# Hybrid decoder trunk on one core: order of a head's score matmuls, and the queues of the first loads

## Chip, cores, metric

The kernel runs on one core of one Trainium2 chip. Its time is the device time of one launch in microseconds (us). Lower is better. The engines are called as in the profile: PE is the matrix engine (TensorE), PEld its weight loads, DVE the vector engine, ACT the scalar engine, POOL is GpSimd, SP the queue engine that issues most DMAs. A line number L927 is a line of the kernel before; the changed kernel has the same lines two or three further down.

## Reference

Two layers of a decoder trunk on x of 512 tokens by 1024. A layer projects RMSNorm(x) once and feeds four branches: a short gated convolution (A), sparse attention with an indexer and top-k (B), a gated linear recurrence in chunks (C), and cross-attention into 256 memory tokens (M). Each branch is lifted to 1024 columns, gated, summed, projected and added to x; a SwiGLU feed-forward follows. What the change touches is the start, where the memory tokens are normed and projected, and the scores inside the recurrence:

```python
def hgrn2_chunkwise(q, k, v, log_f):            # 4 heads, chunks of 64 tokens
    ...
    cum = jnp.cumsum(gc, axis=3)
    ref = cum[:, :, :, HG_CHUNK // 2 - 1:HG_CHUNK // 2, :]
    ...
    a_intra = jnp.einsum('nbhtk,nbhsk->nbhts', qc * jnp.exp(cum - ref), kc * jnp.exp(ref - cum))
    o_intra = jnp.einsum('nbhts,nbhsv->nbhtv', jnp.where(tri, a_intra, 0.0), vc)
    ...
def reference(x, mem, ...):
    mem_n = rmsnorm(mem, mem_norm)
    ...
    mk, mv = jnp.split(mem_n @ mem_w_kv, 2, axis=-1)     # in each layer
```

## The kernel before

**Products.** All large products are made from operands split in two (hi and lo), with three matmuls each: hi by hi (L260), hi by lo (L261), lo by hi (L262). A weight chunk (class Chunk, L212 to L226) is loaded by SP into w_raw, 1 MB for 1024 rows of 256 columns. There are two such buffers. ACT copies it to w_hi (L97 through L224) and DVE subtracts to w_lo (L225), in two halves of 128 by 1024.

**Order.** The order in which engines run their instructions is decided at build time by a scheduler of the tile framework, from dependencies, priorities and estimated times. Each engine then runs its own list strictly in that order. All helpers for ACT are recorded under L97. DMA completions are counted on a small set of semaphores, eight of them for the DMAs of SP and ACT together, handed out in turn; a DMA that gets one in use waits until the earlier DMA on it has landed.

**Start.** SP loads the memory tokens mem_in in one DMA (L150). Parameter rows (norm gains, convolution weights, bounds) are gathered in one tile called rows (L151 to L157): three sets are loaded by ACT's queue (norm_mix, norm_ffn, mem_norm), five by SP's (conv_w, lower bounds, three head norms). Then PE transposes rows once (L160) and ACT copies the result to prm (L161), which holds every gain as a column. Before that PE runs 14 warm-up matmuls (L144).

mem_in_T (L372 to L384) transposes the memory tokens tile by tile (L376), and ACT and DVE write them, scaled by the gain from prm, as mt_hi and mt_lo (L377, L378). ACT squares mem_in for the norm (mem_sq, L381). first_h (L388 to L415) loads x in two halves (xin, L391), squares its four token tiles (mem_sq, L397), and transposes it (L410). mem_kv (L417 to L458) makes keys and values from mt and four weight chunks of a layer; for a chunk and each of two token tiles it runs eight k tiles of three matmuls. It norms keys (L438) and transposes them (L442). The start runs mem_in_T, then mem_kv of layer 0 interleaved with first_h, then mem_kv of layer 1.

**Recurrence.** For each of four heads (function head, L873 to L968) ACT and DVE form the scaled operands, and then PE makes the scores of four 128-token tiles in one PSUM bank pa. A tile holds two chunks of 64. The 128 by 128 product within chunks is L927; the 64 by 64 block between the first chunk of a tile and the second is L928, which overwrites a corner of the same tile:

```python
925  for t in range(NT):
926      s = slice(t * P, (t + 1) * P)
927      pe.matmul(pa[:, s], z[:, s], cmr[:, s], start=True, stop=True)
928      pe.matmul(pa[0:CH, t * P + CH:(t + 1) * P], k_mid[:, t, :], q_mid[:, t, :], start=True, stop=True)
```

These are plain fp32 matmuls, which the profile shows as two passes, each with its weight load. DVE then copies the scores under the causal mask (L930). Behind that stand transposes of the keys (L934), the state updates (L940) and the outputs (L952, L954). The heads are interleaved with logits and with the lift of branch B by a script (L970), so PE has large products between these steps. In attention, L705 multiplies on two half tiles of 64 columns, one in each half of the array.

Of the kernel before, what the change touches and what calls it, by code (L numbers as in the profile page):

```python
# [21 lines left out]
P = 128  # L22
S = 512
NT = S // P
D = 1024
# [44 lines left out]
def hybrid_trunk(ctx: ExitStack, tc: tile.TileContext, x, mem, positions, norm_mix, w_in, conv_w,  # L70
                 dsa_q_norm, dsa_k_norm, hgrn_lower_bounds, hgrn_out_norm, mem_norm, mem_w_kv,
                 mem_q_norm, mem_k_norm, w_lift, w_out, norm_ffn, ffn_w_up, ffn_w_down, out):
    nc = tc.nc
# [29 lines left out]
    def mm_ps():  # L103
        return pmm.tile([P, 512], F32, name="mm")
# [40 lines left out]
    rows = sp.tile([P, P], F32, name="rows")  # L145
# [1 line left out]
    warm = consts.tile([P, 1], F32, name="warm")  # L147
    A(warm, one, AF.Exp)
    mem_in = sp.tile([P, 2, D], F32, name="mem_in")
    nc.sync.dma_start(mem_in, mem[0].rearrange("(t p) d -> p t d", p=P))  # L150
    for lo, src in ((0, norm_mix.rearrange("l (c p) -> (l c) p", p=P)),  # L151
                    (16, norm_ffn.rearrange("l (c p) -> (l c) p", p=P)),
                    (32, mem_norm.rearrange("(c p) -> c p", p=P)),
                    (40, conv_w.rearrange("l w (c p) -> (l w c) p", p=P)),
                    (64, hgrn_lower_bounds.rearrange("l (c p) -> (l c) p", p=P)),
                    (72, hgrn_out_norm), (74, mem_q_norm), (76, mem_k_norm)):
        (nc.scalar if lo < 40 else nc.sync).dma_start(rows[lo:lo + src.shape[0], :], src)  # L157
    prm = consts.tile([P, n_rows], F32, name="prm")
    ps = tr_ps()
    pe.transpose(ps[:, :n_rows], rows[:n_rows, :], ident[:n_rows, :n_rows])  # L160
# [19 lines left out]
    for l in range(DEPTH):  # L180
        a = sp.tile([P, HD], F32, name=f"gq_raw{l}")
# [57 lines left out]
    def pair(a, k, s=slice(None)):  # L239
        return a[0][:, k, s], a[1][:, k, s]  # L240

    def features(w, a, js, k0=0, kt=None, pss=None):
        """Feature-major products of the 128-column tiles js of a chunk."""
        kt = w.kt if kt is None else kt
        pss = [mm_ps() for _ in js] if pss is None else pss
        for ks, _, _ in w.parts:
            for j, ps in zip(js, pss):
                for k in ks:
                    mm3(ps, w.tile(k, j), pair(a, k0 + k), k0 + k == 0, k0 + k == kt - 1)
        return pss  # L250
# [6 lines left out]
    def mm3(ps, a, b, first, last):  # L257
        ah, al = a
        bh, bl = b
        pe.matmul(ps, ah, bh, start=first, stop=False)  # L260
        pe.matmul(ps, ah, bl, start=False, stop=False)  # L261
        pe.matmul(ps, al, bh, start=False, stop=last)  # L262
# [228 lines left out]
    def mixer(l, h, norms, cm, cf):  # L491
# [11 lines left out]
        def lift(n, y, merged, last=None):  # L503
            def gates(m):
                gw = wchunk(w_in[l][:, C_GATE + n * D + m * P:C_GATE + n * D + (m + 2) * P], KD, 256)
                gs = [gate_tile()[:, :S] for _ in range(2)]
                for g, ps in zip(gs, features(gw, h, (0, 1))):
                    with tc.high_priority(offset=AHEAD):
                        dve.tensor_mul(g, ps, r_b)
                    sigmoid(g, g, mix.tile([P, S], F32, name="gate_e", bufs=1))  # L510
                return gs

            look = LOOK[l][n] == "1"
            ahead = gates(0) if look else None
            for m in range(0, KD, 2):
                if look:
                    gs, ahead = ahead, gates(m + 2) if m + 2 < KD else None
                else:
                    gs = gates(m)
                lw = wchunk(w_lift[l, n][:, m * P:(m + 2) * P], 4, 256)  # L520
                pls = features(lw, y, (0, 1))
                for i in range(2):
                    g, pl = gs[i], pls[i]
                    with tc.high_priority(offset=AHEAD):
                        if n == 3:
                            dve.tensor_mul(merged[:, m + i, :], g, pl)
                        else:
                            dve.tensor_mul(g, g, pl)
                            dve.tensor_add(merged[:, m + i, :], merged[:, m + i, :], g)
                    if last is not None:  # L530
                        last(m + i)
                yield
# [26 lines left out]
        def conv_branch(y):  # L559
            for c2 in range(2):  # L560
                us = [gate_tile(), gate_tile()]
                w = wchunk(w_in[l][:, C_AX + c2 * 256:C_AX + (c2 + 1) * 256], KD, 256)
                for u, ps in zip(us, features(w, h, (0, 1))):
                    pool.memset(u[:, 0:2], 0.0)
                    with tc.high_priority(offset=AHEAD):
                        dve.tensor_mul(u[:, 2:], ps, r_b)
                yield
                w = wchunk(w_in[l][:, C_AC + c2 * 256:C_AC + (c2 + 1) * 256], KD, 256)
                for j, ps in enumerate(features(w, h, (0, 1))):
                    c, u = 2 * c2 + j, us[j]  # L570
                    v = gate_tile()[:, :S]
                    with tc.high_priority(offset=AHEAD):
                        dve.tensor_mul(v, ps, r_b)
                    dve.tensor_mul(u[:, 2:], u[:, 2:], v)
                    A(v, u[:, 0:S], AF.Copy, scale=g_conv(l, 0, c))
                    dve.scalar_tensor_tensor(v, u[:, 1:S + 1], g_conv(l, 1, c), v, op0=OP.mult, op1=OP.add)
                    dve.scalar_tensor_tensor(u[:, 2:], u[:, 2:], g_conv(l, 2, c), v, op0=OP.mult, op1=OP.add)
                    dve.tensor_mul(u[:, 2:], u[:, 2:], r_b)
                yield
                w = wchunk(w_in[l][:, C_AB + c2 * 256:C_AB + (c2 + 1) * 256], KD, 256)  # L580
                for j, ps in enumerate(features(w, h, (0, 1))):
                    c, u = 2 * c2 + j, us[j][:, 2:]
                    with tc.high_priority(offset=AHEAD):
                        dve.tensor_mul(u, u, ps)
                    A(y[0][:, c, :], u, AF.Copy)
                    dve.tensor_sub(y[1][:, c, :], u, f(y[0][:, c, :]))
                yield
# [255 lines left out]
        with pool_("hgrn") as hp:  # L843
# [14 lines left out]
            def tmp(name, bufs=HB):  # L858
                return hp.tile([P, S], F32, name=name, bufs=bufs)
# [13 lines left out]
            def head(hh):  # L873
# [51 lines left out]
                for t in range(NT):  # L925
                    s = slice(t * P, (t + 1) * P)
                    pe.matmul(pa[:, s], z[:, s], cmr[:, s], start=True, stop=True)  # L927
                    pe.matmul(pa[0:CH, t * P + CH:(t + 1) * P], k_mid[:, t, :], q_mid[:, t, :], start=True, stop=True)  # L928
                am = a_buf[hh % 2]
                dve.copy_predicated(am, tri[:, None, :].to_broadcast([P, NT, P]),  # L930
# [31 lines left out]
                y, a = tmp("ls"), tmp("ks")  # L962
# [5 lines left out]
                yield  # L968

            script(HG[l], {"z": logits(), "H": chain(*(head(hh) for hh in range(4))), "l": lift(1, y_b, merged)})  # L970
        hvs.close()

# [132 lines left out]
```

## Time and profile before

| | |
|---|---|
| median of three timed runs | 2059.01 us (2058.93 to 2060.22) |
| the profiled execution | span 2057.1 us from first to last instruction; no other time of it is given |
| PE busy | 2046.8 us, 99% of the span |
| PE weight loads busy | 1731.1 us, 84% |
| DVE, ACT busy | 1270.5 us (62%), 1017.1 us (49%) |
| DMA | 203.83 MB, mean 99 GB/s |
| mean granted PE clock | 0.999 |

In the profile's lines an instruction is shown with its line, engine, what it writes and reads, partitions by elements, and times in us, or ns where a mean of one is meant. "x6" is a row of six merged ones: the first start, and the time to the end of the last. An arrow in square brackets names what ended the engine's idle time before it. The waits view sums such idle time: us in total, times, the longest. In the view by stretches each engine's busy time and count stand in order PE, PEld, DVE, ACT, POOL, then PE's granted clock, the share of the DMA engines and GB/s. PE's rows overlap, since matmuls are pipelined: the step from one start to the next is what one costs in a row.

### The profile page before, as it was taken

What the parts mean: (1) busy time and instruction counts of PE and PEld (TensorE: products, weight loads), DVE (VectorE), ACT (ScalarE), POOL (GpSimd) and SP (SyncE); (2) the same over time, 40 slices, a digit from 0 to 9 for tenths busy, and PEclk for the clock granted to TensorE, in tenths of its full rate; (3) what the DMA queues carried; (4) which work ended last, traced back from release to release, by engine and by line L of the source; (5) the groups of instructions that cost most, each with busy time, mean ns of one, the idle gap of its engine ahead of it and who ended that gap; (6) DMA issues with size and microseconds to landing.
All of it is one profiled execution on the core that took longest, in us unless ns stands there. A gap on an engine that the chain in (4) does not pass through costs nothing.

```text
span 2057.1 us, 27077 instructions
## 1 busy us (share of the span) xinstructions
PE 2046.8 (99%) x10588; PEld 1731.1 (84%) x10588; DVE 1270.5 (62%) x2513; ACT 1017.1 (49%) x1836; POOL 9.8 (0%) x33
## 2 busy tenths in 40 slices
PE   8999999999999999999999999999999999999999
PEld 8998988888888888888889898888888888888889
DVE  6779998547676544334457899953766754532542
ACT  7654655856665423223355456576657643322321
POOL 0000000000000000000000000000000000000000
PEclk9999999999999999999999999999999999999999
DMA  7632222212233232232242223321223332322322
GB/s 255 215 95 86 72 89 93 81 53 92 82 113 113 83 102 92 92 114 92 87 154 93 88 75 97 97 66 62 83 82 109 116 102 83 103 93 92 103 72 93
DMA packets 190783, 203.83 MB, mean 99 GB/s; under 512 B 4270, under 2 KB 182528, under 8 KB 190528
## 3 DMA queue, kind: packets, MB, share of 16 engines
q1 hardware_dynamic: 186944, 193.56, 29.2%
q10 hardware_dynamic: 3552, 8.41, 1.1%
q8 instruction: 83, 1.36, 0.3%
q14 instruction: 44, 0.36, 0.1%
q0 software_dynamic: 160, 0.13, 0.0%
HBM read 191.60 MB, written 10.49 MB: 98 GB/s over the span
## 4 chain that ended last, share of the span: by engine, by line
PE 98%; DMA 1%; DVE 0%; ACT 0%; SPq 0%; issue 0%; DVEq 0%; ACTq 0%
PE mm L261 30%; PE mm L260 30%; PE mm L262 30%; PE tr L705 1%; PE tr L699 1%; PE at L676 1%; PE at L675 1%; PE at L927 1%; DMA w_raw<-in_mem_w_kv_dram 1%; PE at L928 0%; PE at L260 0%; PE at L262 0%; PE at L261 0%; PE at L952 0%; PE tr L643 0%; PE tr L744 0%
## 5 line engine op out<-in xcount | busy, mean ns | idle before, releaser
L261 PE MATMUL mm<-h_lo,w_hi 128*128 128x512 f32 x1664 | 652.1, 392 | 0.0
L260 PE MATMUL mm<-h_hi,w_hi 128*128 128x512 f32 x1664 | 651.8, 392 | 0.0
L262 PE MATMUL mm<-h_hi,w_lo 128*128 128x512 f32 x1664 | 649.5, 391 | 0.0
L225 DVE TENSOR_TENSOR w_lo<-w_raw,w_hi 128x1024 fp32r<-128x1024 f32 (+1 forms) x348 | 419.7, 1207 | 350.7 <-ACT w_hi L97 349.5
L97 ACT ACTIVATE w_hi<-w_raw 128x1024 fp32r<-128x1024 f32 (+1 forms) x348 | 363.5, 1046 | 469.6 <-PE mm L261 416.8
L261 PEld LDWEIGHTS mm<-h_lo,w_hi 128*128 128x128 f32 x1664 | 312.6, 188 | 64.9 <-issue 2.5
L262 PEld LDWEIGHTS mm<-h_hi,w_lo 128*128 128x128 f32 x1664 | 312.4, 188 | 65.1 <-issue 1.4
L260 PEld LDWEIGHTS mm<-h_hi,w_hi 128*128 128x128 f32 x1664 | 312.6, 188 | 64.5 <-issue 2.0
L262 PE MATMUL mm<-w_hi,h_lo 128*128 128x256 f32 (+1 forms) x448 | 128.0, 286 | 0.0
L261 PE MATMUL mm<-w_lo,h_hi 128*128 128x256 f32 (+1 forms) x448 | 126.8, 284 | 0.0
L260 PE MATMUL mm<-w_hi,h_hi 128*128 128x256 f32 (+1 forms) x448 | 126.8, 285 | 0.0
L261 PE MATMUL mm<-a_lo,w_hi 128*128 128x512 f32 x272 | 106.1, 390 | 0.0
L260 PE MATMUL mm<-a_hi,w_hi 128*128 128x512 f32 x272 | 105.9, 389 | 0.0
L262 PE MATMUL mm<-a_hi,w_lo 128*128 128x512 f32 x272 | 105.6, 390 | 0.0
L260 PE MATMUL mm<-y_hi,w_hi 128*128 128x512 f32 x256 | 101.3, 397 | 0.0
L262 PE MATMUL mm<-y_hi,w_lo 128*128 128x512 f32 x256 | 100.2, 392 | 0.0
L261 PE MATMUL mm<-y_lo,w_hi 128*128 128x512 f32 x256 | 100.1, 391 | 0.0
L262 PEld LDWEIGHTS mm<-w_hi,h_lo 128*128 128x128 f32 x448 | 85.6, 191 | 1.4 <-issue 0.8
L260 PEld LDWEIGHTS mm<-w_hi,h_hi 128*128 128x128 f32 x448 | 85.2, 191 | 1.2 <-issue 0.8
L261 PEld LDWEIGHTS mm<-w_lo,h_hi 128*128 128x128 f32 x448 | 85.5, 191 | 0.6
L97 ACT ACTIVATE a_hi<-fg 128x512 fp32r<-128x512 f32 x44 | 27.8, 633 | 109.0 <-DVE fg L1054 109.0
L97 ACT ACTIVATE prob<-prob,small 128x128 f32<-128x128 f32 (+3 forms) x128 | 69.2, 555 | 15.2 <-DVE small L688 14.6
(351 smaller groups left out, 3048.6 us busy)
## 6 DMA issues: line engine op xcount, KB each, us to landing
w_raw<-in_w_in_dram SPq DMA_DIRECT2D x72, 1024.0 KB, 5.0
w_raw<-in_ffn_w_up_dram SPq DMA_DIRECT2D x44, 1024.0 KB, 5.1
w_raw<-in_w_lift_dram SPq DMA_DIRECT2D x32, 512.0 KB, 3.4
w_raw<-in_ffn_w_down_dram SPq DMA_DIRECT2D x16, 1024.0 KB, 5.0
w_raw<-in_mem_w_kv_dram SPq DMA_DIRECT2D x8, 1024.0 KB, 5.2
w_raw<-in_w_out_dram SPq DMA_DIRECT2D x8, 1024.0 KB, 4.9
kv<-kv ACTq DMA_DIRECT2D x8, 512.0 KB, 7.4
xT<-x_spill SPq DMA_DIRECT2D x16, 256.0 KB, 5.8
```

The costliest lines, as they stand in the source:

```text
L97: i = act.activation(dst, src, func, **kw)
L225: dve.tensor_sub(lo, raw[:, k:e], f(hi))
L260: pe.matmul(ps, ah, bh, start=first, stop=False)
L261: pe.matmul(ps, ah, bl, start=False, stop=False)
L262: pe.matmul(ps, al, bh, start=False, stop=last)
L675: pe.matmul(ps, q[:, hh, s], k[0][:, :n], start=True, stop=False)
L676: pe.matmul(ps, q[:, hh, s], k[1][:, :n], start=False, stop=True)
L699: pe.transpose(pp[:, (2 * e + i) * P:(2 * e + i + 1) * P], probs[2 * i + e][:, b * P:(b + 1) * P], ident)
L705: pe.matmul(pv[e * HD:(e + 1) * HD, :], vt[:, b, :], pt[:, b, e * 2 * P:(e + 1) * 2 * P], start=b == 0, stop=b == t)
L927: pe.matmul(pa[:, s], z[:, s], cmr[:, s], start=True, stop=True)
```

## The change

The memory tokens are loaded in two DMAs of 512 columns each. Of the parameter rows, ACT's queue now loads five sets (two more: conv_w and the lower bounds) and GpSimd's queue three (the head norms); SP loads none. In the recurrence, a head's four 128-column score matmuls come first, then its four of 64. A docstring is dropped.

```diff
     mem_in = sp.tile([P, 2, D], F32, name="mem_in")
-    nc.sync.dma_start(mem_in, mem[0].rearrange("(t p) d -> p t d", p=P))
+    for hf in range(2):
+        cs = slice(hf * D // 2, (hf + 1) * D // 2)
+        nc.sync.dma_start(mem_in[:, :, cs], mem[0][:, cs].rearrange("(t p) d -> p t d", p=P))
     for lo, src in ((0, norm_mix.rearrange("l (c p) -> (l c) p", p=P)),
                     (16, norm_ffn.rearrange("l (c p) -> (l c) p", p=P)),
                     (32, mem_norm.rearrange("(c p) -> c p", p=P)),
                     (40, conv_w.rearrange("l w (c p) -> (l w c) p", p=P)),
                     (64, hgrn_lower_bounds.rearrange("l (c p) -> (l c) p", p=P)),
                     (72, hgrn_out_norm), (74, mem_q_norm), (76, mem_k_norm)):
-        (nc.scalar if lo < 40 else nc.sync).dma_start(rows[lo:lo + src.shape[0], :], src)
+        (nc.scalar if lo < 72 else nc.gpsimd).dma_start(rows[lo:lo + src.shape[0], :], src)
...
                 for t in range(NT):
                     s = slice(t * P, (t + 1) * P)
                     pe.matmul(pa[:, s], z[:, s], cmr[:, s], start=True, stop=True)
+                for t in range(NT):
                     pe.matmul(pa[0:CH, t * P + CH:(t + 1) * P], k_mid[:, t, :], q_mid[:, t, :], start=True, stop=True)
```

Because the scheduler decides the order, the edits at the start also move instructions that they do not name. In the built changed program the lists of PE, ACT and DVE differ from those before in the first 70 us and, slightly, in the recurrence stages; between these they are the same.

## Prediction

> **What bounds the kernel now.** I read the page first, then TensorE's waits, then the first 25 us of the timeline, then the stretch around the score matmuls.
>
> ```profile
> span 2057.1 us, 27077 instructions
> PE 2046.8 (99%) x10588; PEld 1731.1 (84%) x10588; DVE 1270.5 (62%) x2513; ACT 1017.1 (49%) x1836; POOL 9.8 (0%) x33
> ```
>
> The waits of TensorE over the whole span (engine, who waited for whom, us in total, times, longest):
>
> ```profile
> PE tr L160 <- DMA rows<-in_mem_k_norm_dram: 1.9, 1, 1.9
> PE mm L261 <- DVE w_lo L225: 1.3, 2, 0.8
> PE tr L144 <- DVE ones_d L118: 1.1, 1, 1.1
> PE tr L376 <- DVE mt_lo L378: 0.9, 2, 0.6
> PE mm L260 <- ACT w_hi L97: 0.8, 1, 0.8
> ```
>
> These five are all, and each lies in the first 63 us. From 22 us on TensorE is the bound: microseconds taken out of its queue there shorten the kernel one for one, and a start that is later by some amount moves everything behind it by that amount. So the change has two places: eight blocks of score matmuls (four heads, two layers) in the bound part, and the start.
>
> **The scores.** One block, from its first matmul to what follows it (start, length, instruction; each fp32 matmul is two passes):
>
> ```profile
> 464.63 0.38 PE L927 MATMUL at<-cmr,zf 128*128 128x128 f32 x2
> 465.20 0.49 PE L927 MATMUL at<-cmr,zf 128*128 128x128 f32 x2
> 465.62 0.33 PE L928 MATMUL at<-q_mid,k_mid 128*64 128x64 f32 x2
> 465.88 0.38 PE L927 MATMUL at<-cmr,zf 128*128 128x128 f32 x1
> 467.23 0.55 PE L934 MATMUL tr<-ident,ks 128*128 128x128 f32 x3
> L928 PE MATMUL at<-q_mid,k_mid x64: 222/246/270, 464.9 to 1579.2; 128*64 128x64 f32 x64
> ```
>
> The block takes 467.23 - 464.63 = 2.60. A pair inside it repeats every 465.88 - 465.20 = 0.68: 0.42 for two 128-column passes, 0.26 for two of 64. The second 64 pass ends at 465.95 and lasts at least 0.222, so it starts 0.11 after the first and 0.15 before the next 128 pass. What do such passes cost in a row of their own kind?
>
> ```profile
> 472.63 0.83 PE L940 MATMUL tr<-hv,kst 128*128 128x128 f32 x6
> 414.67 1.08 PE L705 MATMUL tr<-pt,vt 128*64 128x256 f32 x8
> 422.57 1.52 PE L705 MATMUL tr<-pt,vt 128*64 128x256 f32 x12
> ```
>
> Six 128 passes: about 0.28 for the last one leaves 0.55 for five steps, 0.11 each, half of the 0.21 in the mixed order. In the third and second rows, passes on 64-column tiles, four more passes cost 1.52 - 1.08 = 0.44; they run two at a time, so 0.22 a step for 256 columns, twice the 0.11 for 128. Time goes with the columns, so in a row the weight loads lie behind the running passes, for 64-column tiles too. What the mixed order pays is a switch at every change of width: the next load starts only when the last pass has drained.
>
> Grouped, a block is: seven steps of 0.11, the switch 0.21, then for the eight 64 passes a first step of 0.11, six of 0.055 (half of the 128 step; no row shows 64 columns in a row) and 0.15 to switch back: 0.77 + 0.21 + 0.11 + 0.33 + 0.15 = 1.57. That saves 1.03 a block, **8.2 us** for eight. Upper price: if each 64 step keeps its 0.11, the block is 1.90 and the saving 0.70, 5.6 us. The mask copy L930, which waits for the last score, starts no later than before, and TensorE waits for nobody in these stages, so I count the saving in full.
>
> The Trainium skill, "TensorE: Matmul & The Clock Gate", Part 3, says that a weight load overlaps running matmuls only when the row group differs. Both kinds here use all rows, so by that rule no load would hide in either order and the saving would be nothing. The L940 and L705 rows speak against it: the same rows there, and steps without room for a load.
>
> **The start.** The chain of work and the timeline:
>
> ```profile
> 0.81 5.40 DMA mem_in<-in_mem_dram
> 8.08 11.56 DMA w_raw<-in_mem_w_kv_dram
> ```
> ```profile
> SPq L157 <- DMA mem_in<-in_mem_dram: 3.5, 1, 3.5
> ```
> ```profile
> xin<-in_x_dram SPq DMA_DIRECT2D x2, 1024.0 KB, 9.1
> gq_raw<-in_dsa_q_norm_dram POOLq DMA_DIRECT2D x2, 32.0 KB, 5.0
> ```
> ```profile
> 6.50 0.40 SPq L216 DMA_DIRECT2D w_raw<-in_mem_w_kv_dram  x1
> 7.57 0.46 SPq L391 DMA_DIRECT2D xin<-in_x_dram  x1
> 8.47 0.22 ACT L97 ACTIVATE prm<-tr 128x78 f32<-128x78 f32 x1
> 8.80 0.82 ACT L97 ACTIVATE mt_hi<-tr,prm 128x256 fp32r<-128x256 f32 x2
> 11.51 2.00 ACT L97 ACTIVATE w_hi<-w_raw 128x1024 fp32r<-128x1024 f32 x2 [0.70 <-DMA w_raw<-in_mem_w_kv_dram]
> 12.61 0.50 PE L260 MATMUL mm<-w_hi,mt_hi 128*128 128x256 f32 x2 [0.79 <-ACT w_hi L97]
> 16.85 1.06 ACT L97 ACTIVATE mem_sq<-xin 128x1024 f32<-128x1024 f32 x1
> 18.03 1.06 ACT L97 ACTIVATE mem_sq<-xin 128x1024 f32<-128x1024 f32 x1
> 19.09 0.46 ACT L97 ACTIVATE mt_hi<-tr,prm 128x256 fp32r<-128x256 f32 x1
> 22.03 0.39 PE L261 MATMUL mm<-w_lo,mt_hi 128*128 128x256 f32 x1 [0.54 <-DVE w_lo L225]
> ```
>
> SP stands 3.5 us: the last parameter row waits for mem_in (landed 6.2), and behind it are the first weight chunk (lands 11.5), the two halves of x (the second at 7.57 + 9.1 = 16.7) and the second chunk (8.08 + 11.56 = 19.6), each 1 MB. So a chunk takes 19.6 - 16.7 = 2.9 and half of x (16.7 - 11.5)/2 = 2.6. The change empties this queue: the two halves of mem_in, then these four with no row between. In line behind mem_in they land at 6.2 + 2.9 = 9.1, then 11.7, **14.3** and 17.2, some 2.4 us earlier than now. Halving mem_in itself gives nothing: the first square needs both halves.
>
> By itself that would start the products earlier. But ACT's order changes with it. In the built program prm, the one copy that turns the parameter rows into columns, no longer comes before the weight splits; it stands behind three of the four squares of x, the third of which waits for x's second half. And mt_hi, which needs prm, stands behind the fourth. So: x lands 14.3; third square, with prm 1.2 later and the fourth square at 15.6 (spacing 1.18 in the rows, prm slipped in); mt_hi 1.06 after that at 16.7; 0.46 more, and TensorE's first product is at **17.2** instead of 12.6.
>
> Behind it lie the first chunk's 48 products (two token tiles, eight k tiles, three products each) and ten transposes (0.11 each) before the second chunk:
>
> ```profile
> 15.63 0.41 PE L260 MATMUL mm<-w_hi,mt_hi 128*128 128x256 f32 x1
> 15.84 0.41 PE L261 MATMUL mm<-w_lo,mt_hi 128*128 128x256 f32 x1
> 19.77 0.28 PE L260 MATMUL mm<-w_hi,mt_hi 128*128 128x256 f32 x1
> 19.89 0.28 PE L261 MATMUL mm<-w_lo,mt_hi 128*128 128x256 f32 x1
> ```
> ```profile
> 10.00:15.00 5.00, 3.16 (x19) 2.05 (x19) 4.11 (x15) 4.30 (x11) 0.00 (x0) 0.98 1.04 406
> 15.00:18.00 3.00, 3.00 (x16) 3.00 (x16) 2.19 (x12) 2.97 (x7) 0.00 (x0) 0.50 1.06 366
> 18.00:22.00 4.00, 3.49 (x28) 3.29 (x27) 1.73 (x3) 3.86 (x8) 0.00 (x0) 0.97 1.08 339
> ```
>
> At full clock a product steps 0.12: 5.8 + 1.1 = 6.9, so the second chunk starts at 24.1 instead of 22.0, **+2.1**; its split halves have landed by then, so this is TensorE's own work. But the windows show the clock at 0.50 for some 3.4 us after TensorE's thin stretch from 6 to 12.6, with steps of 0.21, back at about 18.2, 5.6 after the restart. Before, that cost little, since TensorE waited for the second chunk anyway. Now the idle stretch is longer and nothing waits at its end. With 4.5 us (between 3.4 and 5.6) at 0.21 instead of 0.12, 4.5 x 0.43 = **+1.9**.
>
> The same page of the Trainium skill, Part 1, has the clock return after one window of about 3.4 us kept busy, the window running free; the 3.4 of the rows agrees. From it I estimate up to 6.8 us at half clock, 2.9 instead of 1.9.
>
> A later place:
>
> ```profile
> 63.90 0.47 DVE L438 TENSOR_SCALAR ku<-ku,mk_r 128x128 f32<-128x128 f32 x2
> 65.72 0.38 PE L442 MATMUL tr<-ident,ku 128*128 128x128 f32 x2
> ```
>
> Here the key transposes come 65.72 - 64.37 = 1.35 us after their operand. In the built program they stand 27 products (27 x 0.12 = 3.2 us) earlier in TensorE's queue, while their norm's steps on ACT and DVE come no earlier among the splits of h and the weights. A wait of 0 to 1.9 us takes the place of the cover; I take **+1.4**.
>
> The other edits I cost at nothing. Two more issues on ACT lie in its wait for mem_in, where the second stands for a row that lands at about 4. GpSimd's three more delay the last row to about 8 (issued near 3, 5.0 to land), and prm stands until 15 for x; if x came at 8 they would decide. Constants behind them are used far later.
>
> **Sum:** -8.2 + 2.1 + 1.9 + 1.4 = -2.8. The profiled execution's span is 2057.1, 1.9 under the median of the timed runs, 2059.0; both should move alike: **2056.2**.
>
> **Rivals.** (1) *The start costs little:* x lands half a microsecond sooner, the clock returns early (+0.7), the transposes keep their cover: 2.1 - 0.5 + 0.7 = +2.3, net -5.9, 2053.1. For it: transfers without a gap; against: the long idle stretch. (2) *64-column steps stay 0.11:* the saving is 5.6, net -0.2, 2058.8. For it: 0.11 is the one step seen for them. (3) *Slower:* grouping frees no load, because in fp32 passes of one bank they never hide; the start's +5.4 stays alone, 2064.4. It decides as soon as a grouped block keeps 1.9 of its 2.60 or more, that is, saves under 5.4 / 8 = 0.68. The L940 row makes it unlikely. (The rule of the Trainium skill quoted above would give this one.) (4) *prm does not hold the start:* products begin 2.4 us earlier as the transfers do, net -8.2 - 2.4 = -10.6, 2048.4. Against it stands ACT's built order.
>
> **Numbers.** Forecast 0.52, (1) 0.25, (2) 0.13, (3) 0.06, (4) 0.04. The forecast's own range is -5 to 0 (start +3 to +8). Leaving out (3) and (4), the range is 2052.5 to 2060.5. 0.2%, about what a measurement of this kernel can tell from no change, is 4.1 us. Faster by more: most of (1), all of (4), a fifth of the forecast: 0.35. Slower by more: (3) and a little of the rest: 0.08. Within: 0.57.
>
> **What would show it.** Right: a score block near 1.57 us, with all four L927 matmuls first; prm near 15.5 on ACT, behind the third square of x; first product near 17; clock 0.5 after it; the second chunk's products near 26; a TensorE wait at the key transposes near 65 to 70. Wrong: prm by 9 us, a block above 1.9, TensorE waits of over a microsecond anywhere behind 75 us, or times above 2060.5.

## The result, and the profile after

The changed kernel takes 2066.28 us (median of six runs, 2065.40 to 2067.20) beside 2059.61 for the kernel before (six runs, 2058.93 to 2060.59): ratio 1.0033, 95% interval 1.0022 to 1.0045. It is slower by some 6.7 us, where the prediction had 2.8 us gained and a range up to 2060.5.

TensorE's waits in the changed kernel, over the whole span (engine, who waited for whom, us in total, times, longest):

```profile
PE tr L378 <- ACT prm L97: 6.2, 1, 6.2
PE mm L262 <- ACT ku L97: 5.9, 1, 5.9
PE tr L162 <- DMA rows<-n_hgrn_lower_bounds_dram: 4.8, 1, 4.8
PE tr L444 <- DVE ku L440: 1.2, 1, 1.2
PE tr L144 <- DVE ones_d L118: 1.1, 1, 1.1
PE mm L262 <- ACT mt_hi L97: 0.7, 1, 0.7
```

Three of these rows are large, and only the first two matter. The third, for the last parameter row, ends before the first, for prm, begins. The second ends at 77 us and was in no step of the prediction.

The score block, whose predicted length was 1.57 us (timeline of TensorE in the changed kernel):

```profile
481.21 1.05 PE L929 MATMUL at<-cmr,zf 128*128 128x128 f32 x8
482.19 0.68 PE L931 MATMUL at<-q_mid,k_mid 128*64 128x64 f32 x8
482.80 0.55 PE L937 MATMUL tr<-ident,ks 128*128 128x128 f32 x3
```

From 481.21 to 482.80 it is 1.59 us, against 2.60 before. All eight blocks are alike. Groups of the two lines, with their mean in ns behind the busy time:

```profile
L929 PE MATMUL at<-cmr,zf 128*128 128x128 f32 x64 | 8.4, 274 | 0.0
L931 PE MATMUL at<-q_mid,k_mid 128*64 128x64 f32 x64 | 5.4, 228 | 0.0
```

To place the rest I match the matmuls of two traces by their order and take the difference of their starts, called lag below. Against the kernel before the lag is +6.7 us from the 100th matmul (29.5 us) to the 400th (65 us), +16.6 from the 550th on, +12.5 after the four score blocks of the first layer and +8.4 at the last matmul. So the score blocks take off 4.1 in each layer, and two places early in the span give 6.7 and 9.9. These are single executions: their spans differ by 7.7 (2064.8 and 2057.1) and the medians by 6.7. I take shares from traces and totals from medians.

The first place, on ACT and then TensorE:

```profile
14.01 1.06 ACT L97 ACTIVATE mem_sq<-xin 128x1024 f32<-128x1024 f32 x1 [1.01 <-DMA xin<-in_x_dram]
16.64 1.06 ACT L97 ACTIVATE mem_sq<-xin 128x1024 f32<-128x1024 f32 x1 [0.31 <-DMA xin<-in_x_dram]
17.70 0.22 ACT L97 ACTIVATE prm<-tr 128x78 f32<-128x78 f32 x1
18.88 0.82 ACT L97 ACTIVATE mt_hi<-tr,prm 128x256 fp32r<-128x256 f32 x2
19.38 0.58 PE L262 MATMUL mm<-w_hi,mt_hi 128*128 128x256 f32 x1 [0.73 <-ACT mt_hi L97]
```

The order is the one that the prediction read from the built program: prm behind the third square, and that behind x's second half. But x lands at 16.6 and not 14.3. Its issues on SP, and the median of their landing:

```profile
2.31 3.08 SPq L393 DMA_DIRECT2D xin<-in_x_dram  x2
```
```profile
xin<-in_x_dram SPq DMA_DIRECT2D x2, 1024.0 KB, 11.6
```

The second place, first the queues (SP and ACT), then the chain of waits, then ACT:

```profile
64.14 6.04 SPq L218 DMA_DIRECT2D w_raw<-in_w_in_dram  x2
64.67 0.34 ACTq L417 DMA_DIRECT2D x_spill<-xc  x1
```
```profile
64.14 11.39 DMA w_raw<-in_w_in_dram
76.67 0.28 ACT ku L97
77.00 0.58 PE mm L262
```
```profile
69.00 0.47 ACT L97 ACTIVATE kv<-mm,mem_r 128x256 fp32r<-128x256 f32 x1 [0.22 <-PE mm L264]
75.62 1.06 ACT L97 ACTIVATE w_hi<-w_raw 128x1024 fp32r<-128x1024 f32 x1 [6.14 <-DMA w_raw<-in_w_in_dram]
76.58 0.37 ACT L97 ACTIVATE ku<-mm 128x256 f32<-128x256 f32 x1
```

ACT's queue issues the 2 MB store of x (x_spill, L417) 0.53 us after SP issues a 1 MB weight chunk. The chunk takes 11.39 us to land (the 72 loads of in_w_in in the page have a median of 5.2). ACT's split w_hi waits 6.14 us for it. Behind the split in ACT's list stands the copy ku, and TensorE waits for that. Then the clock falls again. Stretches of the changed kernel (columns as explained above; the third figure from the end is the granted clock):

```profile
15.00:20.00 5.00, 1.30 (x5) 0.91 (x6) 1.10 (x6) 4.66 (x14) 0.00 (x0) 0.50 1.10 352
20.00:30.00 10.00, 10.00 (x68) 10.00 (x68) 6.70 (x24) 4.57 (x9) 0.00 (x0) 0.77 0.09 29
70.00:80.00 10.00, 3.93 (x18) 3.55 (x19) 4.58 (x17) 3.31 (x11) 0.52 (x1) 0.62 0.91 351
80.00:100.00 20.00, 20.00 (x116) 17.91 (x116) 13.61 (x59) 8.46 (x14) 0.67 (x3) 0.93 0.63 216
```

### The profile page after: what moved, and what is told of

Read it like the earlier page. It is cut to its first block, busy times and chain, and to the rows that moved or that the text cites. A ratio compares the mean times of both kernels' runs of the same rounds, so it can differ in the third digit from the quotient of the medians.

```text
span 2064.8 us, 27090 instructions
## 1 busy us (share of the span) xinstructions
PE 2041.5 (99%) x10588; PEld 1730.8 (84%) x10588; DVE 1271.3 (62%) x2513; ACT 1019.7 (49%) x1836; POOL 11.4 (1%) x36
## 3 DMA queue, kind: packets, MB, share of 16 engines
HBM read 191.60 MB, written 10.49 MB: 98 GB/s over the span
## 4 chain that ended last, share of the span: by engine, by line
PE 98%; DMA 1%; ACT 0%; DVE 0%; issue 0%; ACTq 0%
PE mm L262 30%; PE mm L263 30%; PE mm L264 30%; PE tr L707 1%; PE tr L701 1%; PE at L678 1%; PE at L677 1%; DMA xin<-in_x_dram 1%; DMA w_raw<-in_w_in_dram 1%; PE at L263 0%; PE at L264 0%; PE at L262 0%; PE at L955 0%; PE at L929 0%; PE tr L645 0%; PE tr L746 0%
```

## Experiments

The changed kernel has three working edits: the order of the scores, the queues of the parameter rows, and the memory tokens in halves. Each was timed beside the kernel before on the same chip.

| kernel | median, us | ratio to before, 95% |
|---|---|---|
| scores only | 2051.18 | 0.9962 (0.9950 to 0.9975) |
| both start edits, no scores | 2075.29 | 1.0077 (1.0064 to 1.0090) |
| all edits, store of x held late | 2059.72 | 1.0004 (0.9996 to 1.0013) |
| all edits, prm ordered first | 2055.55 | 0.9983 (0.9974 to 0.9992) |
| queues only | 2068.32 | 1.0042 (1.0029 to 1.0054) |
| scores and halves | 2058.88 | 0.9996 (0.9987 to 1.0005) |
| scores, store held late | 2055.43 | 0.9984 (0.9975 to 0.9993) |
| scores, another start | 2052.50 | 0.9965 (0.9952 to 0.9977) |
| scores and halves, store moved | 2052.76 | 0.9967 (0.9955 to 0.9980) |
| scores and queues | 2060.09 | 1.0002 (0.9993 to 1.0011) |
| scores, prm late | 2058.28 | 0.9995 (0.9986 to 1.0004) |

The kernel before had 2059.18 beside the first four, 2059.53 beside the next four, 2059.51 beside the last three.

**The scores alone.**

```diff
                     pe.matmul(pa[:, s], z[:, s], cmr[:, s], start=True, stop=True)
+                for t in range(NT):
                     pe.matmul(pa[0:CH, t * P + CH:(t + 1) * P], k_mid[:, t, :], q_mid[:, t, :], start=True, stop=True)
```

> The kernel before with the score order alone: four matmuls of 128 columns, then four of 64; the loads as before. Theory A (grouping takes the switches of width away in each of eight blocks, 2.60 to 1.59 us as in the changed kernel, and nothing else moves): 2059.6 - 8.1 = 2051.5 us, blocks of 1.59, start as before (first product near 12.6, clock at half for about 3.4 us). Rival B (the shorter blocks make ACT or DVE late, so that part comes back as waits in the recurrence stages, and the rest of the changed kernel's gain there is due to its shifted order): above 2054.

Measured 2051.18, 8.0 us under the kernel before; the lag at the last matmul is -8.07. It is the fastest version of the study, and beats both kernels.

**Both start edits alone.** The changed kernel with the scores in pairs.

> The kernel before with the edits of the start alone: memory tokens in halves, parameter rows on the queues of ACT and GpSimd; scores paired as before. Theory A (the start's two losses, 6.7 us by 60 us and 9.9 more by 85 us, are all its own): 2059.6 + 16.6 = about 2076 us, and nothing after 90 us differs from before. Rival B (part of the second loss is made up later, or depends on the score order): under 2073.

Measured 2075.29, the sum expected. The lag is +7.4 up to the 400th matmul and +17.1 from the 550th to the end, so the whole loss arises in the first 85 us. The wait for ku (5.9) is there again.

**The store of x out of the way.** In the changed kernel:

```diff
-        nc.scalar.dma_start(x_dram, xc)
...
+    sp_dma = nc.scalar.dma_start(x_dram, xcs)
+    tc.add_manual_dep(sp_dma.ins, last_kv[-1].ins.name, order, reason="spill late")
```

> The changed kernel, with the 2 MB store of x (x_spill) held on ACT's queue until after the last key and value copies of layer 1. Theory A (at 64 us this store shares the DMA engines with the weight chunk of w_in that is issued in the same microsecond, which lands after 11.4 instead of 5 us; TensorE waits 5.9 us for it, and its clock drops for 10 us): that chunk lands in 5 to 6 us, TensorE's wait there is under 1.5 us and the clock stays full there, time 2066.3 - 8 to - 10 = 2056.5 to 2058.5. Rival B (the wait comes from the order alone: the chunk's buffer is freed too late, whatever else is moved): the wait of about 6 us and the second stretch at half clock stay, 2065 to 2067.

Measured 2059.72, 6.6 us better than the changed kernel and 1.2 above what was expected. TensorE's waits:

```profile
PE tr L378 <- ACT prm L97: 5.5, 1, 5.5
PE tr L616 <- ACT sq L97: 1.3, 1, 1.3
PE tr L446 <- DVE ku L442: 1.2, 1, 1.2
```

The wait for ku is gone, and with it the second stretch at half clock. The chunk, issued at 63.85 here, is split 5.2 us later, and ACT does not wait for it:

```profile
69.08 1.05 ACT L97 ACTIVATE w_hi<-w_raw 128x1024 fp32r<-128x1024 f32 x1
```

What stays is 1.2 at the key transposes (L446 here), where the lag goes from +6.4 to +7.5: this is the prediction's +1.4. Right behind them it goes on to +7.9. The store's new place, 76.8 us, costs another 1.4 (lag +7.9 to +9.3, the wait at L616). There the store meets a later chunk, issued 2.03 us behind it (and two 0.5 MB stores go out beside them, at 80.8 and 81.6). ACT's split waits for that chunk, and the squares sq stand behind the split (chain of waits):

```profile
78.84 11.21 DMA w_raw<-in_w_in_dram
```

**prm ahead of the squares of x.** In the changed kernel:

```diff
-            A(mem_sq, xin[:, t, :], AF.Square, scale=D ** -0.5, accum_out=xs[:, t:t + 1])
+            i = A(mem_sq, xin[:, t, :], AF.Square, scale=D ** -0.5, accum_out=xs[:, t:t + 1])
+            tc.add_manual_dep(i.ins, prm_copy.ins.name, order, reason="after prm")
```

> The changed kernel, with the copy of the parameter columns (prm) ordered on ACT ahead of the squares of x; nothing else is held, the rest of the order is the scheduler's. Theory A (the first loss is prm's place behind the third square of x): prm at about 11 to 12.8 us instead of 17.7, first product near 13.5 to 14 instead of 20, the lag by 60 us between 0 and 2 us instead of 6.7; what follows at 65 us depends on the store of x, so 2052 to 2062. Rival B (the start is late because rows and x land late, in whatever order): first product still after 17 us and a lag of 5 us or more.

Measured 2055.55, inside the wide range but with a start lag of 3.9 to 5.0, not 0 to 2. The rows explain it:

```profile
13.12 0.22 ACT L97 ACTIVATE prm<-tr 128x78 f32<-128x78 f32 x1
```
```profile
PE tr L162 <- DMA rows<-n_hgrn_lower_bounds_dram: 4.2, 1, 4.2
```

With x out of its way prm still comes at 13.12, because the last parameter row now lands after 10 us and ACT then makes a weight split first. The store (60.2) and the next chunk (62.5) lie 2.3 us apart in this order, and no wait of TensorE stands behind them.

**The queues alone.** The kernel before with one line changed:

```diff
-        (nc.scalar if lo < 40 else nc.sync).dma_start(rows[lo:lo + src.shape[0], :], src)
+        (nc.scalar if lo < 72 else nc.gpsimd).dma_start(rows[lo:lo + src.shape[0], :], src)
```

> The kernel before with only the queues of the parameter rows changed (ACT's queue five sets, GpSimd's three); the memory tokens stay in one load and the scores in pairs. Theory: the queues alone move prm behind the squares of x in ACT's built order, so the whole loss of the start comes from them: prm at 16 to 19 us, first product at 18 to 20, a first half-clock stretch of 10 us or more, and, if the store of x again meets a weight load near 64 us, 2068 to 2077. Rival, the halves of the memory tokens do the harm: within 2 us of the kernel before, about 2059.

Measured 2068.32: +8.8 from this line alone. prm comes at 21.18, behind all four squares and a split; the store of x (64.2) goes out 2.3 us ahead of the next chunk (66.5) and TensorE waits for nothing there.

**The halves, with the scores.**

```diff
-    nc.sync.dma_start(mem_in, mem[0].rearrange("(t p) d -> p t d", p=P))
+    for hf in range(2):
+        cs = slice(hf * D // 2, (hf + 1) * D // 2)
+        nc.sync.dma_start(mem_in[:, :, cs], mem[0][:, cs].rearrange("(t p) d -> p t d", p=P))
```

> The kernel before with the grouped scores and the memory tokens in two loads; the queues of the parameter rows as before. Theory: the halves cost nothing, prm stays at 8.5 us and the first product at 12.5: 2051.2 as with the scores alone, give or take 1. Rival: the halves delay mem_in's last landing and the queue behind it, or bring the store of x onto a weight load: 2053 or more, with a first product past 13.5 us or a wait of TensorE near 65 us.

Measured 2058.88, 7.7 above the scores alone: my theory, that the halves cost nothing, fell. prm comes at 8.89 and the first product at 13.0, so a late prm is not it. The lag against the scores alone is 1.8 at the 400th matmul and 7.3 from the 550th. The 1.8 arises between 23 and 29 us, where the granted clock is at half from 23.9 to 27.4 us; in the kernel with the scores alone it is full by then. The other 5.5 arise later. For these, queue of ACT, chain of waits, ACT, and TensorE's waits of this kernel:

```profile
54.00 0.41 ACTq L417 DMA_DIRECT2D x_spill<-xc  x1
```
```profile
54.08 10.49 DMA w_raw<-in_mem_w_kv_dram
```
```profile
51.34 1.07 ACT L97 ACTIVATE w_hi<-w_raw 128x1024 fp32r<-128x1024 f32 x1
64.67 1.06 ACT L97 ACTIVATE w_hi<-w_raw 128x1024 fp32r<-128x1024 f32 x1 [6.47 <-DMA w_raw<-in_mem_w_kv_dram]
```
```profile
PE tr L444 <- DVE ku L440: 3.7, 1, 3.7
PE mm L262 <- ACT w_hi L97: 1.5, 1, 1.5
```

And the same split and load in the kernel with the scores alone:

```profile
47.09 1.06 ACT L97 ACTIVATE w_hi<-w_raw 128x1024 fp32r<-128x1024 f32 x1
```
```profile
49.43 0.37 SPq L216 DMA_DIRECT2D w_raw<-in_mem_w_kv_dram  x1
```

The halves change the scheduler's order. On ACT the second split of a chunk slips behind copies of x (51.34 instead of 47.09), so its buffer comes free 4.7 us later and the next chunk is issued at 54.08 instead of 49.43. That is 0.08 us after the store of x, and the chunk takes 10.49 us to land.

**The scores, with the store held late.** The edit of the store above, in the kernel with the scores alone.

> The kernel before with the grouped scores and with the store of x held behind the last value copy of the second layer's memory keys and values; the start as before. A control for the run that held the store back in the changed kernel: theory, the store costs nothing where it meets no weight load that TensorE waits for, so moving it away gives 2051.2, give or take 1, and the 6.5 us that it gave in the changed kernel were the collision. Rival, the late store is a gain by itself: 2048 or less.

Measured 2055.43, 4.3 worse than the scores alone, so as a control it failed. The store goes out at 69.3 us, and TensorE then waits for a load of the keys (its waits, and the chain of waits):

```profile
PE at L260 <- DMA mk<-kv: 1.5, 1, 1.5
```
```profile
77.34 9.61 DMA mk<-kv
```

That the store is what slows this load was not tried by itself.

A late store is thus no gain by itself, and the 6.6 us that it gave in the changed kernel are net of such a price.

**Another start.** The scores, the head-norm rows alone on GpSimd's queue, and prm ordered ahead of the first splits and of x's squares.

> The kernel before with the grouped scores, the three head-norm rows alone moved to GpSimd's queue (two stay on SP, three on ACT), and prm ordered on ACT ahead of the first weight splits and of x's squares. Theory: with SP free of the row that waited 3.5 us for the memory tokens, the first weight chunk lands near 9 to 10.5 instead of 11.5 us, and with prm at 8.5 to 10 the first product comes at 10.5 to 12: 2049 to 2051.2. Rival: the rows of GpSimd's queue land late (near 10.6, as in the changed kernel), prm at 11 or later, first product 12.5 or later, 2051 to 2055.

Measured 2052.50, with the first product at 13.81: the rival's time, but not by its step. TensorE waits 2.6 us for the rows, and prm comes at 9.54, where the theory had it. But the first chunk is split only at 11.39, not at 9 to 10.5, and the copies mt_hi stand behind that split (13.30). No gain over the scores alone.

**One store moved.** In the kernel with scores and halves the store alone moves, a few places down ACT's list:

```diff
-        nc.scalar.dma_start(x_dram, xc)
...
+    with tc.high_priority(offset=AHEAD):
+        sp_dma = nc.scalar.dma_start(x_dram, xcs)
+    tc.add_manual_dep(sp_dma.ins, splits[13].ins.name, order, reason="spill after a split")
```

> The run with grouped scores and halved memory tokens, with one instruction moved: the store of x goes behind the next weight split on ACT, from 54.0 to about 57.9 us, so that it no longer starts together with the weight chunk of 54.1 us. Theory: that chunk's 10.5 us to landing were the shared transfer; alone it lands in about 5, ACT's wait of 6.5 us and TensorE's wait of 3.7 us at the key transposes go, and the time falls from 2058.9 to 2052 to 2055 (some is given back by the chunk of 59.3 us, which now shares with the store). Rival, the wait has another cause (the order of the splits behind the rope tables): 2058 to 2060 and the chunk still lands after 10 us.

Measured 2052.76: 6.1 us from one instruction. Queues of SP and ACT, then ACT:

```profile
54.17 0.37 SPq L220 DMA_DIRECT2D w_raw<-in_mem_w_kv_dram  x1
```
```profile
55.95 0.34 ACTq L468 DMA_DIRECT2D x_spill<-xc  x1
59.69 1.06 ACT L97 ACTIVATE w_hi<-w_raw 128x1024 fp32r<-128x1024 f32 x1 [1.40 <-DMA w_raw<-in_mem_w_kv_dram]
```

The chunk goes out at 54.17, as in the run with the store in its place (54.08), and is there at 59.7 instead of 64.7. The store follows it by 1.8 us (I had expected 3.7), and the 3.7 us at the key transposes are gone. So it was the meeting, and not the order of the splits, that cost.

**The changed kernel without the halves.** Scores and queues.

> The changed kernel with the memory tokens in one load again: grouped scores and the new queues of the parameter rows. Theory, the parts add: 2068.3 of the queues alone less 8.1 of the scores is 2060.2; prm near 21 us, no wait of TensorE near 65 us. So the halves of the memory tokens cost the changed kernel some 6 us, by the meeting of the store and a weight chunk. Rival, the meeting comes from the queues as well, once the scores are grouped: 2066 or more.

Measured 2060.09, as the sum of the parts said. So in the changed kernel the halves cost 6.2 us (2066.28 - 2060.09). That is a net figure: without them prm stands behind the fourth square and a split as well (20.71), and the start alone lags 9.6 us and not 6.7, but no meeting follows.

**prm late, every load as before.**

```diff
+            if t == 2:
+                tc.add_manual_dep(prm_copy.ins, i.ins.name, order, reason="prm late")
```

> The kernel before with grouped scores, and prm ordered on ACT behind the third square of x, as in the changed kernel; every load on its queue of before. Theory, the place of prm alone makes the late start: x lands at 16.7, prm at 17.9, first product at 19 to 20, a lag of 6 to 8 us against the run with the scores alone: 2057.5 to 2059.5 where the store meets no chunk. Rival, the late rows and transfers of the new queues make it: first product before 15 us, 2051 to 2054.

Measured 2058.28, 7.1 above the scores alone (8.4 in its trace, which is of the slowest of eleven runs), with prm and the first product as in the changed kernel:

```profile
18.18 0.22 ACT L97 ACTIVATE prm<-tr 128x78 f32<-128x78 f32 x1
```
```profile
19.87 0.58 PE L260 MATMUL mm<-w_hi,mt_hi 128*128 128x256 f32 x1 [0.73 <-ACT mt_hi L97]
```

The queue line costs 8.9 with the scores (2060.09 - 2051.18), and prm's place alone makes 7.1 of a loss of that kind.

## Why the prediction was wrong, by its steps

| step | predicted, us | measured, us |
|---|---|---|
| score blocks | -8.2 | -8.1 (traces), -8.0 (medians) |
| start, to the second chunk | +2.1 and +1.9 | +6.7 |
| key transposes | +1.4 | +1.1 |
| other edits: halves, store | 0 | +8.8 (9.9 less the 1.1) |
| sum | -2.8 | +8.5 in the traces, +6.7 in the medians |

**The score blocks were right**, term by term. In the rows above, eight 128 passes step (1.05 - 0.27) / 7 = 0.11; the switch is 482.19 - 481.21 - 0.78 = 0.20; the 64 passes step (0.68 - 0.23) / 7 = 0.064 where 0.055 was taken; the switch back is 0.16. Rivals 2 and 3, that the 64 steps stay at 0.11 or that grouping frees no load, are out. The trace's weight loads show the switch itself: within the row the load for the next pass starts with the running pass (both at 481.32), and at the change of width it starts 0.20 us after the last 128 pass (482.19 and 481.99). One more rival was not named: a 64 block overwrites a corner that its 128 passes have just written, so the paired order might have paid for that and not for the width. The switch costs 0.20 in either order, though in the grouped one the first corner was written 0.9 us earlier; so it is the change of width. The Trainium skill, "TensorE: Matmul & The Clock Gate", Part 3, has loads overlap only where the row group differs; both kinds of matmul use all rows here, and the grouped block is 1.01 us shorter all the same, so here the measurement decides against the rule.

**The start had the right mechanism and one mis-sized input.** The prediction put x's second half at 14.3, as a queue of transfers one behind another. In the changed kernel SP issues x's first half at 2.3 and its second at 5.0 (the row above), ahead of before (6.9 and 7.6), but each takes 11.6 us to land where it took 9.1, and the second half lands when it did before. By ACT's waits mem_in is there at 6.50, the first chunk at 10.57 and the halves of x at 14.01 and 16.64: steps of 4.1, 3.4 and 2.6, where the prediction's queue had 2.9, 2.6 and 2.6. From 8 to 10 us the DMA engines are as busy as before (1.07 and 1.00), but move 259 GB/s and not 345. The rest follows the prediction's steps: prm 1.1 after the third square, mt_hi 1.2 after prm, the first product 0.5 after that, at 19.4 instead of 17.2. The clock is at half from the restart to 24.6 (10 us at a mean of 0.77 are 4.6 at half), so 5.2 x 0.43 = 2.2 instead of 1.9. Then 2.1 + 2.2 + 2.2 = 6.5, beside the 6.7 of the lag. That prm's place makes such a start is shown by the run that moves prm alone; why x lands no sooner was not tried, nor the clock's share by itself. The Trainium skill, the same page, Part 1, has full clock return after one busy window of about 3.4 us; the prediction's estimate from it, up to 6.8, holds the 5.2 measured.

**The edit that it costed at nothing was the larger fault.** "Halving mem_in itself gives nothing" is true of the transfer, but the prediction followed the built order for prm and the key transposes alone, and not the DMAs on ACT's list. The store of x had moved to within 0.5 us of a weight chunk that an ACT split, and behind it ku, wait for. Before, they are 2.6 us apart, the store first, ACT needs the chunk only 8.2 us after its issue, and no wait of TensorE follows (ACT's queue, SP's, ACT):

```profile
55.13 0.34 ACTq L415 DMA_DIRECT2D x_spill<-xc  x1
57.70 0.37 SPq L216 DMA_DIRECT2D w_raw<-in_w_in_dram  x1
65.93 1.05 ACT L97 ACTIVATE w_hi<-w_raw 128x1024 fp32r<-128x1024 f32 x1
```

The prediction had looked at ACT's queue at the start alone, and named TensorE waits of over a microsecond past 75 us as the sign of an error; this one runs from 71 to 77. Of its 8.8 us, 5.9 are the wait; the 5.7 us at half clock from 77.0 on cost about 5.7 x 0.43 = 2.5, reckoned as at the start.

**The parameter rows**, costed at nothing while prm waits for x, were covered as said: 4.8 us of wait end before prm does. But the last row is not one of GpSimd's three, near 8 us; it is the lower bounds on ACT's queue, and TensorE has it at 10.8. With the cover gone (prm ordered first) the late row shows, and prm comes at 13.1 and not 9. Rivals 1 and 4 failed on prm and on x's landing.

## What to carry to other kernels

When a scheduler orders the program, an edit is costed by the whole difference of the built orders up to the point where the lists agree again: for each DMA that moved, look at what else is in flight beside it, which engine waits for that, and how soon. An edit worth nothing by itself can move a large store onto the load that the next product needs; here one store, a few places up or down ACT's list, was worth 6.1 us. Group matmuls of one width: the gain was the number of width switches saved, and it came out as worked from the rows.

## What the runs showed of the hardware

A 1 MB load that is issued within about half a microsecond of a 2 MB store on another queue took 10.49 us (store 0.08 us ahead) and 11.39 us (store 0.53 us behind) to land. With the store 1.8 us behind it was used after 5.5. A load 2.03 us behind the store took 11.21 (the changed kernel with the store held late; smaller stores went out beside it, and their share was not tried). With the store 2.3 to 2.6 us ahead of the load no wait of TensorE over 0.4 us followed (the kernel before, the queues alone, prm first); there ACT took the chunk more than 8 us after its issue, so these runs do not show when it landed. The Trainium skill, "DMA: Bandwidth & Descriptors", "Issuing engines are not separate DMA queues", says that transfers of different queues run on the same engines and interleave; these runs agree, and in one of them a head start of 1.8 us over the store was enough for the load to be spared. Where between 0.5 and 1.8 it turns was not tried.

A DMA on ACT's list can go out before the arithmetic that stands ahead of it has begun: in the run with one store moved it is issued at 55.95, while the split just ahead of it in the built list starts at 56.94.

In the trace's clock record of the changed kernel the granted clock is at half for 13.65 us in the start (11.04 to 24.70) and for 10.24 us around the second wait (72.48 to 82.72). Both are whole multiples of 3.41 us, the length of the one such stretch in the start of the kernel before (14.85 to 18.26). From the first product after the wait to full clock it is 5.3 us at the first place (5.2 by the stretches shown) and 5.7 at the second.
